# An eighth set of seven block products over x in a gated hybrid trunk: a linear-attention gate group and a merge gate are computed as a set of their own

## The chip, the cores and the metric

The kernel runs on one core of one Trainium2 chip. The metric is the device time of one execution in microseconds (us). A core has a matrix engine (TensorE, PE in the profile, with its weight loads as PEld), a vector engine (VectorE, DVE), a scalar engine (ScalarE, ACT), GpSimd (POOL) and SyncE (SP), which here only issues transfers. The engines run side by side, each works its instructions in order, and they wait for each other by semaphores. Sixteen DMA engines move data between the memory of the chip (HBM) and the on-chip memory.

## The reference, cut to what matters

One layer on x (256 tokens, 2048 channels, float32). It is a normalisation, one wide projection, two token mixers side by side, and two more projections:

```
h = rmsnorm(x, pre_norm_g)
proj = h @ w_in            # 2048 x 18448 columns
a_q, a_k, a_v, a_g, a_lr, b_q, b_k, b_v, b_g, m_a, m_b = split(proj)
gk  = log_sigmoid(a_lr @ gla_gk_w2 + gla_gk_b) / 16
o_a = rmsnorm(gla(a_q, a_k, a_v, gk)) * silu(a_g)       # linear attention, 4 heads
o_b = rmsnorm(diff_attention(b_q, b_k, b_v)) * (1 - lam_init) * silu(b_g)   # 16 heads
merged = sigmoid(m_a) * (o_a @ w_branch_a) + sigmoid(m_b) * (o_b @ w_branch_b)
out = x + rmsnorm(merged @ w_out, post_norm_g)
```

The change touches the columns a_g (the gate of linear attention, 2048 wide, four groups of 512) and m_b (the merge gate of the second branch, four groups of 512). What is computed does not change.

## The kernel before, in words

**Precision.** Every weight and every left operand is split into two float32r parts: hi, made by ScalarE, and lo, what is left over, made by VectorE. A product is the sum of three matmuls: hi with hi, lo with hi, hi with lo.

**Blocks.** `chunk_plan` lists the blocks of columns. Most are 512 columns wide: `v*` (values of linear attention), `ag0` to `ag3` (its gate), `dv*` and `bg*` (values and gate of differential attention), `m00` to `m13` (merge gates), `y*` (the two branch projections), `o*` (the output). The keys and queries (`k*`, `q*`, `dk*`, `dq*`) are 128 columns each. Weights are streamed from HBM in halves of 128 x 1024 floats (512 KB), and each half is used once.

A **plain** token-major block (`token_major`) is 8 halves; each gives 12 matmuls of 512 columns: 2 slices of the contraction, 2 halves of the tokens, 3 products. A channel-major block (`channel_major`, keys and queries) is 2 halves.

**Sets.** Two 512-column blocks can be computed together as a 2 x 2 block product with seven instead of eight block products (the scheme of Strassen and Winograd). `SETS` names the pairs, `PRODUCTS` the seven products with their operand (a quarter of x or a sum of quarters, "square"), their chain and the weight quarter that is added. A product has 4 **units**, a set 28; a unit is one half of weights and 6 matmuls (`set_product`). The sums of weight quarters are built in **chains**: buffers in the on-chip memory into which GpSimd's queue loads one quarter (L233) and then adds the next by an accumulating DMA (L232). `refill` issues each such load two units after the buffer was read. A set in `MOVED` takes the order of `ORDERS[0]`, where all chain sums are made by DMA and the quarter of p2 comes by SP; the other sets use `ORDERS[1]`, in which VectorE adds two buffers for four units after p5 (L255) and four at p2 (L260). `FULL` marks a set that loads the quarter of p2 late, by SP. Sets 0 and 1 begin with empty chains (`start_sets`); later sets are chained to the one before.

The results of a set go to `head_set` (values and gate of a group of four heads), `merge_gate` (tanh, then a store to HBM) or the output.

**Order.** `schedule` writes the order of all halves and units: `regular` puts plain blocks, `mixed(n, ...)` spreads n units evenly among the halves of the blocks named. `take` hands out the next half or unit and keeps four of them emitted ahead; hi and lo have three buffers each. Everything else is a list of **tasks** (generators: the scores and the output of linear attention, differential attention, fetches), and `pump` advances the first of them by a step after every second unit, every channel block, or every second half of a plain block (every half while `fast` is set). A planner then orders the instructions of each engine by what it expects them to cost; `keep_in_program_order` pins some. The pool `big` has 34 tiles of 4 KB a partition, shared by operands, chains, values and attention.

**Stages, by the profile's times.** v blocks, then v4 with keys and queries and set 0 (to 234 us); ag0 to ag3, with the last levels of the linear attention's scores and its output step `gla_out` (to 353); four head stages, each with 16 halves of dq and dk, units between, and differential attention (`diff_attention`) as tasks (to 669); m12 and m13; y0, the first branch (from 744); y1; o2 with the last set; o3 and the end.

`gla_out(hf)` runs once for each pair of heads of linear attention. It needs the scores, the values of its two heads (`vh`, `vl`, stored to HBM earlier and fetched by `fetch_values`) and two gate tiles (`ua`). `gates_of` and `values_of` hold the results of a head set until differential attention has used them; `weigh` waits until the set of its group is complete. After the head stages `fetch_a` brings back the operands of y0 (`oah`, `oal`).

Of the kernel before, what the change touches and what calls it, by code (L numbers as in the profile page):

```python
# [79 lines left out]
def schedule():  # L80

    kinds = {key: kind for key, kind, _, _ in chunk_plan()}
    steps = []
    blocks = [(i, n) for i in range(len(SETS)) for n in range(SLOTS * 4)]

    def regular(*keys):
        steps.extend((key, n) for key in keys for n in range(units(kinds[key])))

    def mixed(n, *keys):
        at = len(steps)  # L90
        regular(*keys)
        r = steps[at:]
        del steps[at:]
        for i, step in enumerate(r):
            steps.extend(blocks[: (i + 1) * n // len(r) - i * n // len(r)])
            del blocks[: (i + 1) * n // len(r) - i * n // len(r)]
            steps.append(step)

    def channels(g):
        return [key for key in kinds if key[:2] in ("dq", "dk") and key[2] == str(g)]  # L100

    order = [key for key, _, _, _ in chunk_plan()]
    def alone(n):
        steps.extend(blocks[:n])
        del blocks[:n]

    regular(*order[: order.index("v4")])
    mixed(SLOTS * 4, *order[order.index("v4") : order.index("ag0")])
    regular("ag0", "ag1")
    mixed(5, "ag2")  # L110
    mixed(8, "ag3")
    mixed(15, *channels(0))
    mixed(19, *channels(1))
    mixed(20, *channels(2))
    mixed(20, *channels(3))
    mixed(18, "m12", "m13")
    mixed(43, *(f"y0{g}" for g in range(4)))
    alone(4)
    mixed(16, "y10", "y11")
    regular("y12", "y13")  # L120
    mixed(SLOTS * 4, "o2")
    regular("o3")
    assert not blocks
    return steps


SLOTS = 7
SETS = (("dv0", "bg0"), ("dv1", "bg1"), ("dv2", "bg2"), ("dv3", "bg3"), ("m10", "m11"), ("m00", "m01"), ("m02", "m03"), ("o0", "o1"))
LAST = 6
OUT = 7  # L130


PRODUCTS = {
# [7 lines left out]
}  # L141


MOVED = (0, 2, 3)

FULL = (4,)
ORDERS = (("p1", "q3", "p5", "p2", "q6", "q7", "p4"), ("p1", "q3", "p5", "q6", "q7", "p2", "p4"))


# [4 lines left out]
def order_of(n):  # L154
    return OUT_ORDER if n == OUT else ORDERS[n not in MOVED]

# [9 lines left out]
def hybrid_kernel(ctx: ExitStack, tc, xt, xn, preg, postg, w, w2, gkb, glag, lamv, diffg, ident_d, causal_d, lmask_d, out):  # L166
# [107 lines left out]
    def emit_half():  # L274
        j = emitted[0]
        emitted[0] += 1
        key, unit = steps[j]
        if j in begin:
            start_sets()
        if j == begin_out:  # L280
            start_out()
        if j == begin_out + 8:
            for n in range(4):
                plain[OUT, "p2", n] = u([P, 1024], "plain")
                block(OUT, "p2", n, add=False)
        if isinstance(key, int):
            i = set_steps.index((key, unit))
            name, part = order_of(key)[unit // 4], unit % 4
            if key == 1 and part == 0 and unit < 16:
                fetch_square(PRODUCTS[order_of(key)[unit // 4 + 1]][0])  # L290
            chain, (kh, g) = chain_of(key, name), PRODUCTS[name][2]
            if (key, name, part) in plain:
                raw = plain.pop((key, name, part))
            elif chain is None:
                raw = wpool.tile([P, 1024], F32, tag="raw", name=f"raw_s{key}_{unit}", bufs=6)
                at = 1024 * (part % 2)
                sp.dma_start(raw, piece(SETS[key][g], 2 * kh + part // 2)[:, at : at + 1024])
            else:
                raw = chains[chain][part]
            hi_t = wpool.tile([P, 1024], F32R, tag="hi", name=f"hi_{j}")  # L300
            lo_t = wpool.tile([P, 1024], F32R, tag="lo", name=f"lo_{j}")
            act.activation(hi_t, raw, AF.Copy)  # L302
            dve.tensor_tensor(out=lo_t, in0=raw, in1=f32(hi_t), op=ALU.subtract)  # L303
            refill(i, key, name, part, raw)
            ready[j] = ((key, unit), hi_t, lo_t)
            return
        size = sizes[key]
        h = unit % 2
        src = piece(key, unit // 2)
        n = size // 2  # L310
        early = key == "v0"
        if j == 2:
            load_x(2, 2)
        if j == 0:
            raw = raw_0
        else:
            raw = wpool.tile([P, 1024], F32, tag="raw", name=f"raw_{key}_{unit}", bufs=6)
            i = sp.dma_start(raw[:, :n], src[:, n * h : n * h + n])
        if early:
            if j:  # L320
                tc.keep_in_program_order(i)
            if j == 0:
                load_x(1, 1)
            for kt in X_LOADS[j // 2] if h else ():
                load_x(kt, 4)
        if early:
            prep_x(j)
            if 6 <= j < 14:
                square_x(j - 6)
        if key == "o3" and j + 1 < len(steps):  # L330
            hi_t, lo_t = u([P, 1024], "keep", F32R), u([P, 1024], "keep", F32R)
        else:
            hi_t = wpool.tile([P, 1024], F32R, tag="hi", name=f"hi_{j}")
            lo_t = wpool.tile([P, 1024], F32R, tag="lo", name=f"lo_{j}")
        fine = 2 if j == 0 else 1
        for i in range(fine):
            a, b = n * i // fine, n * (i + 1) // fine
            r = raw[:, a:b]
            act.activation(hi_t[:, a:b], r, AF.Copy)  # L339
            dve.tensor_tensor(out=lo_t[:, a:b], in0=r, in1=f32(hi_t[:, a:b]), op=ALU.subtract)  # L340
        ready[j] = (key, hi_t, lo_t)
# [350 lines left out]
    def fetch_square(name):  # L692
        parts[name] = tuple(u([P, 8, P], "square", F32R) for _ in range(2))
        for t, src in zip(parts[name], parts_far[name]):
            tc.keep_in_program_order(pool.dma_start(f32(t), src))
# [76 lines left out]

    values_of, gates_of = {}, {}

    def head_set(n, src, i, b):
        g = n
        if i == 0:
            if b == 0:
                values_of[g] = u([P, 2, 512], "dv")
            act.activation(values_of[g][:, b, :], src, AF.Copy, scale=rstd[:, b : b + 1])  # L780
        else:
            if b == 0:
                gates_of[g] = u([P, 2, 512], "ub")
            gate(src, b, gates_of[g][:, b, :])

    def all_sets():
        for n in range(4):
            yield from block_set(n, lambda src, i, b: head_set(n, src, i, b))
            done.add(f"set{n}")
        yield from block_set(4, lambda src, i, b: merge_gate(1, i, b, src))  # L790
        for n in (5, 6):
            yield from block_set(n, lambda src, i, b: merge_gate(0, 2 * n - 10 + i, b, src))
        yield from out_set()

    def fetch(dst, src):
# [134 lines left out]
    def gla_out(hf, gates):  # L930
        og = []
        while f"scores{hf}" not in done:
            yield
        fetch_values(2 * hf + 1)
        for h in range(2):
            (ah, al), xh_, xl_ = att[hf], vh[2 * hf + h], vl[2 * hf + h]
            banks = [ps("bg"), ps("bg")]
# [12 lines left out]
            for b in range(2):  # L950
                dve.scalar_tensor_tensor(out=o[:, b, :], in0=banks[b], scalar=ssq[:, b : b + 1], in1=o[:, b, :], op0=ALU.mult, op1=ALU.mult)
            og.append(o)
            yield
            if h == 0 and not fast[0]:
                yield
# [18 lines left out]
    def fetch_values(h):  # L974
        vh[h], vl[h] = u([P, 2, 512], "vh", F32R), u([P, 2, 512], "vl", F32R)
        for t, far in ((vh[h], vh_far[h]), (vl[h], vl_far[h])):
            tc.keep_in_program_order((pool if h == 3 else sp).dma_start(f32(t), far))

    gates = []
    for g in range(4):  # L980
        if g % 2:
            fetch_values(g - 1)
        fast[0] = True
        banks = token_major(f"ag{g}", 512, x_ops)
        fast[0] = False
        t = u([P, 2, 512], "ua")
        for b in range(2):
            gate(banks[b], b, t[:, b, :])
        gates.append(t)
        if g % 2:  # L990
            tasks.insert(0 if f"scores{g // 2}" in done else len(tasks), gla_out(g // 2, gates[g - 1 :]))


    obh, obl = [], []
# [75 lines left out]
    def diff_attention():  # L1070

        last = pair = og = None
        n = 0
        while n < 16 or last or pair:
            new = None
            if n < 16:
# [44 lines left out]
            last = new  # L1121
            if n == 16:
                yield

    def diff_heads(g):
        obh.append(u([P, 4, S], "obh", F32R))
# [24 lines left out]

    tasks.append(diff_attention())
    diff_heads(0)
    while not {"out0", "out1"} <= done:
        pump()
    diff_heads(1)
    diff_heads(2)
    diff_heads(3)

# [14 lines left out]
            yield  # L1174

    tasks.append(fetch_a())
    for g in (2, 3):
        banks = token_major(f"m1{g}", 512, x_ops, 2)
        for b in range(2):
            merge_gate(1, g, b, banks[b])  # L1180
    while tasks:
        pump()
    for g in range(4):
# [296 lines left out]
```

## Time and profile before

| | us |
|---|---|
| median of three runs | 1098.16 |
| lowest and highest | 1097.91, 1099.25 |
| profiled execution, whole | 1099.57 |
| profiled execution, span from first to last instruction | 1097.8 |

| engine | busy us | share |
|---|---|---|
| PE | 1086.1 | 99% |
| PEld | 930.2 | 85% |
| DVE | 863.6 | 79% |
| ACT | 692.5 | 63% |
| POOL | 195.7 | 18% |

The mean granted clock of TensorE is 0.998 of full speed. The DMA queues read 266.22 MB from HBM and wrote 24.12 MB over the span.

How to read it: a row of a group names the line, the engine, the operation, output and input tiles, the shape and the count, then the busy time with the mean duration in ns, then the idle time of the engine before these instructions and what ended it. A matmul's row shows about 390 ns for 512 columns because matmuls are pipelined; the distance between their starts is what they cost when they follow each other.

### The profile page before, as it was taken

What the parts mean: (1) busy time and instruction counts of PE and PEld (TensorE: products, weight loads), DVE (VectorE), ACT (ScalarE), POOL (GpSimd) and SP (SyncE); (2) the same over time, 40 slices, a digit from 0 to 9 for tenths busy, and PEclk for the clock granted to TensorE, in tenths of its full rate; (3) what the DMA queues carried; (4) which work ended last, traced back from release to release, by engine and by line L of the source; (5) the groups of instructions that cost most, each with busy time, mean ns of one, the idle gap of its engine ahead of it and who ended that gap; (6) DMA issues with size and microseconds to landing.
All of it is one profiled execution on the core that took longest, in us unless ns stands there. A gap on an engine that the chain in (4) does not pass through costs nothing.

```text
span 1097.8 us, 15522 instructions
## 1 busy us (share of the span) xinstructions
PE 1086.1 (99%) x5504; PEld 930.2 (85%) x5504; DVE 863.6 (79%) x1193; ACT 692.5 (63%) x1009; POOL 195.7 (18%) x291
## 2 busy tenths in 40 slices
PE   9999999999999999999999999999999999999997
PEld 9999888888888888888888888788888888888886
DVE  6787668997779697877887787877778687687994
ACT  7868555655656566776766776656565666536772
POOL 0112103000211211302221211312111223201100
PEclk9999999999999999999999999999999999999999
DMA  8789989857899768989799879898787999987874
GB/s 318 257 294 332 301 278 259 314 171 269 235 359 244 268 204 233 227 234 291 220 218 307 239 219 300 224 337 305 212 236 233 328 346 349 363 307 233 209 194 149
DMA packets 83262, 291.37 MB, mean 265 GB/s; under 512 B 10032, under 2 KB 11056, under 8 KB 83184
## 3 DMA queue, kind: packets, MB, share of 16 engines
q0 software_dynamic: 34528, 124.80, 43.7%
q1 hardware_dynamic: 47792, 164.31, 42.0%
q10 hardware_dynamic: 864, 1.27, 0.3%
q8 instruction: 43, 0.70, 0.2%
q14 instruction: 35, 0.29, 0.1%
HBM read 266.22 MB, written 24.12 MB: 264 GB/s over the span
## 4 chain that ended last, share of the span: by engine, by line
PE 96%; issue 1%; DVE 1%; DMA 0%; POOL 0%; ACT 0%; DVEq 0%; POOLq 0%; SPq 0%; ACTq 0%
PE mm L510 36%; PE set L710 27%; PE mm L531 16%; PE mm L533 8%; PE bg L510 2%; PE mm L492 1%; PE bg L1012 1%; PE bg L886 1%; PE bg L492 1%; PE bg L1045 0%; PE bg L1223 0%; PE bg L1101 0%; PE bg L963 0%; DMA raw_first<-in_w_dram 0%; PE bg L1052 0%
## 5 line engine op out<-in xcount | busy, mean ns | idle before, releaser
L302 ACT ACTIVATE hi<-chain 128x1024 fp32r<-128x1024 f32 x188 | 198.9, 1059 | 158.3 <-PE mm L531 61.3
L303 DVE TENSOR_TENSOR lo<-chain,hi 128x1024 fp32r<-128x1024 f32 x188 | 229.2, 1223 | 87.3 <-ACT hi L302 85.9
L531 PE MATMUL mm<-xs,hi 128*128 128x512 f32 x768 | 198.3, 391 | 0.0
L531 PEld LDWEIGHTS mm<-xs,hi 128*128 128x128 f32 x768 | 143.4, 188 | 28.4 <-DVE oal L546 0.3
L232 POOL DMA_DIRECT2D chain<-in_w_dram x96 | 83.6, 877 | 400.9 <-DVE lo L303 257.8
L510 PE MATMUL mm<-hi,xs 128*128 128x512 f32 (+2 forms) x640 | 152.0, 377 | 0.8 <-ACT hi L339 0.8
L510 PEld LDWEIGHTS mm<-hi,xs 128*128 128x128 f32 x640 | 119.8, 190 | 16.3 <-ACT hi L339 1.1
L710 PE MATMUL set<-hi,square 128*128 128x512 f32 x448 | 122.8, 395 | 0.0
L533 PEld LDWEIGHTS mm<-xs,lo 128*128 128x128 f32 x768 | 104.7, 190 | 7.4
L533 PE MATMUL mm<-xs,lo 128*128 128x256 f32 x768 | 107.2, 282 | 0.0
L340 DVE TENSOR_TENSOR lo<-raw_y,hi 128x1024 fp32r<-128x1024 f32 x64 | 78.3, 1224 | 31.7 <-ACT hi L339 31.7
L339 ACT ACTIVATE hi<-raw_y 128x1024 fp32r<-128x1024 f32 x64 | 67.9, 1060 | 53.0 <-PE mm L510 33.9
L710 PEld LDWEIGHTS set<-hi,square 128*128 128x128 f32 x448 | 81.3, 189 | 15.9 <-ACT qk L1134 1.0
L710 PE MATMUL set<-hi,xs 128*128 128x512 f32 x336 | 92.0, 395 | 0.0
L510 PE MATMUL mm<-lo,xs 128*128 128x512 f32 (+2 forms) x320 | 82.2, 375 | 0.0
L710 PEld LDWEIGHTS set<-hi,xs 128*128 128x128 f32 x336 | 60.8, 189 | 11.7 <-ACT qk L1134 1.3
L710 PE MATMUL set<-lo,square 128*128 128x512 f32 x224 | 69.5, 391 | 0.0
L510 PEld LDWEIGHTS mm<-lo,xs 128*128 128x128 f32 x320 | 60.1, 189 | 8.1 <-DVE lo L340 0.3
L233 POOL DMA_DIRECT2D chain<-in_w_dram x64 | 35.4, 562 | 155.7 <-DVE lo L303 114.0
L339 ACT ACTIVATE hi<-raw_ag 128x1024 fp32r<-128x1024 f32 x32 | 34.0, 1061 | 33.2 <-PE mm L510 19.3
L710 PE MATMUL set<-lo,xs 128*128 128x512 f32 x168 | 51.9, 390 | 0.0
L510 PE MATMUL mm<-hi,obh 128*128 128x512 f32 x128 | 50.1, 392 | 0.0
(301 smaller groups left out, 1980.4 us busy)
## 6 DMA issues: line engine op xcount, KB each, us to landing
chain<-in_w_dram POOLq DMA_DIRECT2D x160, 512.0 KB, 8.8
raw_y<-in_w_dram SPq DMA_DIRECT2D x64, 512.0 KB, 6.7
raw_ag<-in_w_dram SPq DMA_DIRECT2D x32, 512.0 KB, 4.9
raw_dq<-in_w_dram SPq DMA_DIRECT2D x32, 512.0 KB, 6.0
raw_dk<-in_w_dram SPq DMA_DIRECT2D x32, 512.0 KB, 6.8
raw_v<-in_w_dram SPq DMA_DIRECT2D x31, 416.0 KB, 5.2
raw_k<-in_w_dram SPq DMA_DIRECT2D x16, 512.0 KB, 7.4
raw_q<-in_w_dram SPq DMA_DIRECT2D x16, 512.0 KB, 7.9
```

The lines of the kernel that those rows point to most:

```text
L232: return pool.dma_start(dst, src, accum_op=ALU.add)
L233: return queue.dma_start(dst, src)
L302: act.activation(hi_t, raw, AF.Copy)
L303: dve.tensor_tensor(out=lo_t, in0=raw, in1=f32(hi_t), op=ALU.subtract)
L339: act.activation(hi_t[:, a:b], r, AF.Copy)
L340: dve.tensor_tensor(out=lo_t[:, a:b], in0=r, in1=f32(hi_t[:, a:b]), op=ALU.subtract)
L492: i = pe.matmul(out, lhs, rhs, start=first and n == 0, stop=last and n == len(pairs) - 1)
L510: i = pe.matmul(banks[g][b][:, :n], a[part][:, P * b : P * b + P], w[:, c : c + n], start=first, stop=last)
L531: i = pe.matmul(o, hi[:, c], x_pair(kt), start=kt == 0, stop=kt == KT - 1)
L533: i = pe.matmul(o[:, :S], lo[:, c], x_ops(kt)[0], start=False, stop=False)
L710: i = pe.matmul(bank, a[part], wt[:, 512 * j : 512 * j + 512], start=go, stop=end, skip_group_check=not first)
L886: pe.matmul(o, xk[:, P * c : P * c + P], xq.rearrange("p (b c t) -> p b c t", b=2, c=4)[:, :, c, :], start=i == 0, stop=i == 1)
```

## The change

- `SETS` gets a new first pair, ("ag3", "m13"). The plain blocks ag3 and m13 disappear from the order. `first_set` takes the new set's results: the gate tile `linear_gate` for the last head of linear attention, and `merge_gate(1, 3, ...)`.
- All other sets move one place back; `LAST`, `OUT`, `MOVED` and `FULL` are renumbered with them, so that each old set keeps its order of products, and the set that is now second (dv0, bg0) begins with empty chains. The squares are fetched back for it in its own order of products.
- The order has 4 and 6 units in ag1 and ag2, 26, 28, 28, 28 in the head stages, 14 in m12 and 42 in y0, instead of 5 and 8 in ag2 and ag3, 15, 19, 20, 20, then 18 in m12 and m13, and 43.
- `gla_out(1)` is queued after ag2. It fetches the values of head 2 itself, takes two more steps before it uses them, and fetches those of head 3 (on GpSimd's queue) only after head 2 is done.
- `diff_attention` does not start before both halves of linear attention have their output; the loop that forced this after the first head stage is gone. After the last scores it takes one more step.

```diff
@@ schedule
-    regular("ag0", "ag1")
-    mixed(5, "ag2")
-    mixed(8, "ag3")
-    mixed(15, *channels(0))
-    mixed(19, *channels(1))
-    mixed(20, *channels(2))
-    mixed(20, *channels(3))
-    mixed(18, "m12", "m13")
-    mixed(43, *(f"y0{g}" for g in range(4)))
+    regular("ag0")
+    mixed(4, "ag1")
+    mixed(6, "ag2")
+    mixed(26, *channels(0))
+    mixed(28, *channels(1))
+    mixed(28, *channels(2))
+    mixed(28, *channels(3))
+    mixed(14, "m12")
+    mixed(42, *(f"y0{g}" for g in range(4)))
@@
-SETS = (("dv0", "bg0"), ("dv1", "bg1"), ("dv2", "bg2"), ("dv3", "bg3"), ("m10", "m11"), ("m00", "m01"), ("m02", "m03"), ("o0", "o1"))
-LAST = 6
-OUT = 7
+SETS = (("ag3", "m13"), ("dv0", "bg0"), ("dv1", "bg1"), ("dv2", "bg2"), ("dv3", "bg3"), ("m10", "m11"), ("m00", "m01"), ("m02", "m03"), ("o0", "o1"))
+LAST = 7
+OUT = 8
-MOVED = (0, 2, 3)
-FULL = (4,)
+MOVED = (0, 1, 3, 4)
+FULL = (5,)
@@ emit_half
-            if key == 1 and part == 0 and unit < 16:
-                fetch_square(PRODUCTS[order_of(key)[unit // 4 + 1]][0])
+            if key == 1 and part == 0 and unit < 24:
+                ahead = PRODUCTS[order_of(key)[unit // 4 + 1]][0]
+                if ahead in parts_far:
+                    fetch_square(ahead)
@@
+    linear_gate = []
+
+    def first_set(src, i, b):
+        if i:
+            merge_gate(1, 3, b, src)
+            return
+        if b == 0:
+            linear_gate.append(u([P, 2, 512], "ua"))
+        gate(src, b, linear_gate[0][:, b, :])
@@ all_sets
-        for n in range(4):
-            yield from block_set(n, lambda src, i, b: head_set(n, src, i, b))
-            done.add(f"set{n}")
-        yield from block_set(4, lambda src, i, b: merge_gate(1, i, b, src))
-        for n in (5, 6):
-            yield from block_set(n, lambda src, i, b: merge_gate(0, 2 * n - 10 + i, b, src))
+        yield from block_set(0, first_set)
+        for g in range(4):
+            yield from block_set(g + 1, lambda src, i, b: head_set(g, src, i, b))
+            done.add(f"set{g}")
+        yield from block_set(5, lambda src, i, b: merge_gate(1, i, b, src))
+        for n in (6, 7):
+            yield from block_set(n, lambda src, i, b: merge_gate(0, 2 * n - 12 + i, b, src))
@@ gla_out
-        fetch_values(2 * hf + 1)
+        fetch_values(hf + 1)
+        if hf:
+            yield
+            yield
...
             og.append(o)
+            if h == 0 and hf:
+                fetch_values(3)
             yield
@@
-    for g in range(4):
-        if g % 2:
-            fetch_values(g - 1)
+    for g in range(3):
+        if g == 1:
+            fetch_values(0)
...
-        if g % 2:
-            tasks.insert(0 if f"scores{g // 2}" in done else len(tasks), gla_out(g // 2, gates[g - 1 :]))
+        if g:
+            tasks.insert(0 if f"scores{g - 1}" in done else len(tasks), gla_out(g - 1, gates[:2] if g == 1 else (gates[2], linear_gate[0])))
@@ diff_attention
+        while "out1" not in done:
+            yield
         while n < 16 or last or pair:
...
             if n == 16:
                 yield
+                yield
@@
     diff_heads(0)
-    while not {"out0", "out1"} <= done:
-        pump()
     diff_heads(1)
+    assert {"out0", "out1"} <= done
...
-    for g in (2, 3):
-        banks = token_major(f"m1{g}", 512, x_ops, 2)
-        for b in range(2):
-            merge_gate(1, g, b, banks[b])
+    banks = token_major("m12", 512, x_ops, 2)
+    for b in range(2):
+        merge_gate(1, 2, b, banks[b])
```

More of the change, by code (lines that the diff above doesn't have):

```diff
@@ L773, in hybrid_kernel, with head_set @@
     values_of, gates_of = {}, {}
-    def head_set(n, src, i, b):
-        g = n
+    linear_gate = []
[6 more added lines that the diff above has]
+        gate(src, b, linear_gate[0][:, b, :])
+    def head_set(g, src, i, b):
         if i == 0:
```

## The prediction

> **What bounds the kernel now.** I read the page first: busy shares and the chain that ended last.
>
> ```profile
> span 1097.8 us, 15522 instructions
> ...
> PE 1086.1 (99%) x5504; PEld 930.2 (85%) x5504; DVE 863.6 (79%) x1193; ACT 692.5 (63%) x1009; POOL 195.7 (18%) x291
> ...
> PE 96%; issue 1%; DVE 1%; DMA 0%; POOL 0%; ACT 0%; DVEq 0%; POOLq 0%; SPq 0%; ACTq 0%
> ```
>
> TensorE is busy for 99% of the span and is 96% of the chain. Its waits on other engines, with their total, number and longest, are few:
>
> ```profile
> PE bg L1101 <- DVE ogb L1068: 1.4, 1, 1.4
> PE bg L425 <- DVE ones L422: 1.1, 1, 1.1
> PE mm L510 <- ACT hi L339: 0.8, 1, 0.8
> ```
>
> So what counts is how many matmuls are issued and how far apart. The chain in order of time gives the distance:
>
> ```profile
> 710.40 2.72 PE mm L510 x12
> ...
> 737.60 2.72 PE set L710 x12
> ...
> 1083.34 7.33 issue
> ```
>
> Twelve 512-column matmuls take 2.72 us in a plain block and in a set alike: 0.2267 us each. The 7.33 us at the end follow the last product and are not touched.
>
> The third view is the time by stretch: four head stages, then the block m12, then the branch stage y0, y1, and the stage of the last set (busy time of each engine, granted clock, share of the 16 DMA engines, GB/s).
>
> ```profile
> core 0: us, PE busy (x) PEld busy (x) DVE busy (x) ACT busy (x) POOL busy (x), PEclk, DMA share, GB/s
> 353.50:427.90 74.40, 74.40 (x410) 63.58 (x409) 61.39 (x97) 47.34 (x78) 12.54 (x21) 1.00 0.75 248
> 427.90:503.00 75.10, 75.10 (x426) 64.30 (x425) 58.05 (x122) 51.38 (x99) 16.90 (x20) 1.00 0.91 234
> 503.00:583.00 80.00, 80.00 (x452) 68.58 (x451) 64.64 (x131) 54.25 (x103) 19.07 (x27) 1.00 0.89 240
> 583.00:669.00 86.00, 86.00 (x483) 73.64 (x482) 67.36 (x130) 58.61 (x107) 17.17 (x24) 1.00 0.88 252
> 669.00:706.00 37.00, 37.00 (x187) 30.58 (x186) 32.17 (x64) 25.23 (x51) 5.69 (x6) 1.00 0.83 255
> 744.00:886.00 142.00, 142.00 (x627) 117.40 (x626) 104.99 (x92) 86.18 (x92) 28.36 (x45) 1.00 0.87 268
> 896.00:957.00 61.00, 61.00 (x270) 50.48 (x269) 45.44 (x42) 34.98 (x36) 17.16 (x29) 1.00 1.03 345
> 1015.00:1067.00 52.00, 52.00 (x231) 42.79 (x230) 51.74 (x55) 40.57 (x49) 6.79 (x8) 1.00 0.83 203
> ```
>
> TensorE is full in every row. The last row matters most: VectorE is at 51.74 of 52.00 us and TensorE still loses nothing, so a VectorE share in the nineties is no loss in itself.
>
> **The main term.** A plain 512-column block is 8 halves of 12 matmuls, so ag3 and m13 are 2 x 96 = 192. A set is 28 units of 6, or 168. The change removes 24: 24 x 0.2267 = **5.44 us**, all on the path. Every other matmul stays and only changes place.
>
> The Trainium skill, page "TensorE: Matmul & The Clock Gate", section "Back-to-back issue gap", states a sustained spacing of about 131 ns at 512 columns; by it the term would be an estimated 3.1 us. The trace disagrees with its 0.2267 us.
>
> **What the set adds beside TensorE.** 28 halves are split into hi and lo instead of 16, so 12 more of each of these:
>
> ```profile
> L302 ACT ACTIVATE hi<-chain 128x1024 fp32r<-128x1024 f32 x188 | 198.9, 1059 | 158.3 <-PE mm L531 61.3
> L303 DVE TENSOR_TENSOR lo<-chain,hi 128x1024 fp32r<-128x1024 f32 x188 | 229.2, 1223 | 87.3 <-ACT hi L302 85.9
> ...
> L232 POOL DMA_DIRECT2D chain<-in_w_dram x96 | 83.6, 877 | 400.9 <-DVE lo L303 257.8
> ```
>
> ACT gets 12 x 1.06 = 13 us, VectorE 12 x 1.22 = 15 us and six sums of a bank, about 4 us; GpSimd 24 more issues of at most 0.88 us, 21 us. Shares become 65%, 81% and 20%. SP loses 16 loads and gains four. All of this is hidden on average; the question is where it bunches. The new set itself runs where the first set runs now, with the same 28 units among the same blocks. Each later set starts one place later, and the plain blocks that are gone leave more units for the head stages: 26, 28, 28, 28 instead of 15, 19, 20, 20, and 14 beside the one block m12 instead of 9.
>
> The split's share of VectorE in two of the stretches:
>
> ```profile
> 503.00:583.00 80.00, 43.14 (x37) 1.00 0.89 240
> ...
> 669.00:706.00 37.00, 19.41 (x17) 1.00 0.83 255
> ```
>
> 37 splits take 43.14 us, 1.17 each; the rest of VectorE there is 64.64 - 43.14 = 21.5 us. With 44 halves (16 + 28) the stage has 80 + 7 x 1.36 = 89.5 us of TensorE and 64.64 + 7 x 1.17 = 72.8 us of VectorE, 81%. The stage of heads 1 also gets the eight chain sums of the unmoved set dv1, which now falls there:
>
> ```profile
> L255 DVE TENSOR_TENSOR chain<-chain,chain 128x1024 f32<-128x1024 f32 x4 | 4.9, 1218 | 0.0
> ```
>
> 8 x 1.22 = 9.8, with 1.5 us for the larger part of a set's own sums: 84.1 of 89.5 us, 94%. In m12 (17 halves become 22): TensorE 37 + 5 x 1.36 + about 1 us of attention's end = 44.8; VectorE 32.17 + 5 x 1.14 + two more chain sums 2.4 + the set's sums and attention's end, some 3.6 = 43.9, 98%. Both lie below the 99.5% that costs nothing between 1015 and 1067 us. Attention works beside them, though, in bursts. Bounds: 0, and 7.2 us (the first rival). I take 0.5, nearer to the rows in which TensorE is full.
>
> **The linear attention's end.** It comes into the first head stage, without ag3 to cover it. The values of head 2 are now fetched when the output step begins, two task steps ahead of their product. Those steps are worth about 6.8 us there (three units of 1.36 and a half of 2.72), and such loads land after:
>
> ```profile
> DMA to landing us min/median/max: 5.0/7.4/9.7
> ```
>
> TensorE works in order, so it would wait between 0 and 9.7 - 6.8 = 2.9 us, once; the matmul may also have been placed later by the planner. I take 0.5. Attention now waits for this output. Counted task step by task step with 2.72 us a half and 1.36 us a unit, the output is complete some 11 us later than now, and the first scores only 3 us later, since more units mean more steps. From then on each head's set ends ahead of the first product that needs it, so that wait stays empty.
>
> **m12 and the start of y0.** In the trace m12 starts at 668.97 and the plain m13 gives room behind it:
>
> ```profile
> 668.97 1.98 PE L510 MATMUL mm<-hi,xs 128*128 128x512 f32 x8
> ...
> 708.42 0.59 PE L1101 MATMUL bg<-ident,ogb 128*128 128x128 f32 x2 [1.43 <-DVE ogb L1068]
> ...
> 744.24 0.39 PE L510 MATMUL mm<-hi,oah 128*128 128x512 f32 x1
> ```
>
> Attention ends 39.5 us after m12's start, y0 begins after 75. Now m12 alone lasts 8 x 2.72 + 14 x 1.36 = 40.8 and some 4 us of attention, so y0 begins at about 45, and its fifth load, which first needs the third and fourth fetched operand, at 45 + 4 x (2.72 + 1.31 x 1.36) = 63. These are SP's fetches (start and length of each, then landing):
>
> ```profile
> 696.74 0.37 SPq L796 DMA_DIRECT2D oah<-oah_far  x1
> ...
> 708.65 0.32 SPq L796 DMA_DIRECT2D oal<-oal_far  x1
> ...
> DMA to landing us min/median/max: 9.9/12.3/22.3
> ```
>
> 28 to 40 us after m12's start, landed by 52 at the median and 62 at worst: just in time. Behind a late fetch on SP stand the weight halves of y0. Bounds: -1.4 (the wait at 708 goes) and +5; I take 0.2.
>
> **Transfers.** The bytes moved now:
>
> ```profile
> DMA packets 83262, 291.37 MB, mean 265 GB/s; under 512 B 10032, under 2 KB 11056, under 8 KB 83184
> ```
>
> Twelve more halves of 512 KB are 6.3 MB, 2%. A chain's buffer is refilled eight units later: 8/28 x 89.5 = 25.6 us in the head stages, against 8/43 x 142 = 26.4 in y0, whose row shows TensorE full. Landing of chain loads:
>
> ```profile
> DMA to landing us min/median/max: 3.8/8.8/21.0
> ```
>
> I take 0 here.
>
> **Sum.** -5.44 + 0.5 + 0.5 + 0.2 = -4.2 us on the profiled execution: its span 1097.8 becomes 1093.6. It took 1099.57 us as a whole, 1.4 above the median of the three runs; I put the difference on the median: 1098.16 - 4.2 = **1093.9**.
>
> **Rivals.** *VectorE bunches at the chain sums.* While four units carry a sum each, the head stage has 4 x 1.36 + 2.29 x 2.72 = 11.7 us of TensorE and (8 + 2.29) x 1.22 + 0.27 x 11.7 = 15.7 us of VectorE: 4.0 too much. Now, in m12 (3.56 halves to four units), it is (8 + 3.56) x 1.22 + 0.21 x 15.1 = 17.3 against 4 x 1.36 + 3.56 x 2.72 = 15.1: 2.2 too much, and no wait shows there until 708. Beyond 2.2 it could cost 1.8, at four places (twice in heads 1, twice at m12): 7.2 us, **1099.9**; with nothing absorbed 16, 1108.7. Against it: the hi and lo buffers run two units ahead, and not every sum is urgent.
>
> *A late fetch* of values or operands at both of the places above: 2.9 + 5 - 0.7 on the forecast, **1101** at worst, 1097 at half.
>
> *Transfers become the bound of the head stages*, the case on the other side. Each of heads 1 to 3 must move 44 halves and two stores of 0.52 MB, 24.1 MB in 89.5 us: 270 GB/s. Heads 0 moves 42 and some 12 other such tiles (values in, operands in and out), 28.3 MB in 74.4 + 11 x 1.36 + about 5 us of linear attention = 94 us: 301 GB/s. If 234 / 0.91 = 257 GB/s were the ceiling, these stages would take 93.8 and 110 us: 3 x 4.3 + 16 = 29 us, **1122**. It decides from the point where the rate stays below 270. Against it: 345 GB/s between 896 and 957 us with TensorE full. The Trainium skill, page "Perfetto Trace Analysis", section "Identifying the Most-Contended Engine", says that occupancy misleads for the DMA engines and bytes should be judged; by this the share of 0.91 is no ceiling. The trace agrees with its 1.03 at 345 GB/s.
>
> *More is won*: the wait of 1.4 us goes and nothing comes, 1098.16 - 5.44 - 1.4 = 1091.3.
>
> **How the numbers follow.** Forecast 0.62 (1092 to 1095.9); bunching 0.17, of it 0.05 beyond 1100.4; late fetch 0.07; transfers 0.09; more won 0.05. A measurement of this kernel tells about 0.2%, 2.2 us, from no change. Faster: 0.62 + 0.05 = 0.67. Same: 0.12 + 0.07 = 0.19. Slower: 0.05 + 0.09 = 0.14. The range runs from 1091.3 to 1100.0, which leaves out transfers and the worst bunching.
>
> **What would show it.** Matmuls 5480 instead of 5504; TensorE's busy time down by 5.4 us; 12 matmuls at 2.72 us as now; TensorE full in heads 1 and m12 with VectorE above 90%; no wait of TensorE on vh or oah. I am wrong if TensorE's waits in the head stages or around y0's start sum to over 3 us, or if the chain leaves TensorE for DMA or VectorE there.

## The result and the profile after

The changed kernel takes 1109.52 us (median of 4 runs, 1106.76 to 1111.48) against 1098.70 us for the kernel before on the same chip: a ratio of 1.0093, interval 1.0079 to 1.0107. It is slower by 10.8 us. The forecast was 1093.9, faster by 4.2, with a range that ended at 1100.0.

The page of the changed kernel, its span, busy shares and the chain that ended last:

```profile
span 1108.2 us, 15525 instructions
...
PE 1085.6 (98%) x5480; PEld 925.9 (84%) x5480; DVE 879.0 (79%) x1211; ACT 708.6 (64%) x1023; POOL 217.9 (20%) x315
...
PE 38%; DVE 2%; issue 1%; ACT 1%; DMA 0%; DVEq 0%; POOLq 0%; POOL 0%; ACTq 0%
```

The 24 matmuls are gone (5480 instead of 5504), and the shares of the other engines lie within two points of the ones worked out beforehand (79%, 64% and 20% against 81%, 65% and 20%). Yet the busy time of TensorE fell by 0.5 us only, not by 5.4. So two things happened: TensorE waited more, and while it was busy, it was slower somewhere. The named engines of the chain now sum to 42% of the span, so the time is read from the waits and the stretches instead.

The waits of TensorE in the changed kernel (total, number, longest):

```profile
PE set L712 <- ACT p L729: 4.0, 1, 4.0
PE mm L533 <- ACT hi L341: 3.5, 5, 0.9
PE bg L494 <- DMA vl<-vl_far: 3.0, 1, 3.0
PE bg L427 <- DVE ones L424: 1.1, 1, 1.1
PE mm L512 <- ACT hi L341: 1.0, 2, 0.7
PE set L712 <- ACT hi L304: 0.6, 1, 0.6
PE mm L535 <- DVE lo L342: 0.6, 2, 0.4
```

Three rows are new and large. None of the three names VectorE.

**First, the fetch of values.** TensorE in the output step `gla_out(0)`, then the queue of SP at the same place, both from the timeline (start, length):

```profile
294.50 0.61 PE L712 MATMUL set<-hi,square 128*128 128x512 f32 x2
298.14 0.50 PE L494 MATMUL bg<-vl,ath 128*128 128x512 f32 x1 [3.03 <-DMA vl<-vl_far]
...
299.25 0.63 PE L494 MATMUL bg<-vh,atl 128*128 128x512 f32 x1
299.68 0.63 PE L494 MATMUL bg<-vh,ath 128*128 128x512 f32 x1
```

```profile
289.93 0.33 SPq L994 DMA_DIRECT2D vh<-vh_far  x1
290.35 0.38 SPq L994 DMA_DIRECT2D vl<-vl_far  x1
```

The values of head 1 are fetched at 290, and the second of the two transfers lands 7.7 us after its issue, at 298. SP's own waits say why it was not issued earlier:

```profile
SPq L994 <- PE bg L494: 2.9, 1, 2.9
```

SP waited until TensorE had read head 0's values: there was no free tile in the pool. In the kernel before these two loads went out at 276.6 and 277.1, ahead of the matmuls of head 0, which began at 283.6.

**Second, the copy of a set's product.** ScalarE and TensorE in m12, from the timeline:

```profile
713.72 0.50 ACT L1047 ACTIVATE prob<-prob,mx,score_scale 128x128 f32<-128x128 f32 x1 [0.27 <-DVE mx L1042]
...
714.47 1.07 PE L512 MATMUL mm<-lo,xs 128*128 128x512 f32 x4
...
718.84 0.18 ACT L1047 ACTIVATION_READ_ACCUMULATOR prob<-prob,mx,score_scale 128x1 f32 x1
718.93 0.57 ACT L729 ACTIVATE p<-set 128x512 f32<-128x512 f32 x1
719.55 2.08 PE L712 MATMUL set<-hi,square 128*128 128x512 f32 x4 [4.02 <-ACT p L729]
721.43 1.05 PE L712 MATMUL set<-lo,square 128*128 128x512 f32 x2
```

In the order of a set that is not moved, q6 follows p5 directly and accumulates on p5's bank, after ScalarE has copied that bank out (L729). ScalarE has the exponentials of two heads ahead of this copy, from 713.72 to 718.93, with one split among them. TensorE stands still for 4.0 us.

**Third, the first operand of a half in the head stages**, at one of five places:

```profile
481.21 0.49 ACT L1047 ACTIVATE prob<-prob,mx,score_scale 128x128 f32<-128x128 f32 x1 [0.61 <-DVE mx L1042]
...
486.34 0.19 ACT L1047 ACTIVATION_READ_ACCUMULATOR prob<-prob,mx,score_scale 128x1 f32 x1
486.43 1.04 ACT L341 ACTIVATE hi<-raw_dq 128x1024 fp32r<-128x1024 f32 x1
487.53 1.66 PE L533 MATMUL mm<-xs,hi 128*128 128x512 f32 x6 [0.67 <-ACT hi L341]
```

Again the exponentials of two heads, 5.2 us with one split between, stand ahead of what TensorE needs next.

The waits alone do not make up the loss. The stretches around the first two show the rest (busy time of each engine, granted clock of TensorE, share of the DMA engines, GB/s):

```profile
core 0: us, PE busy (x) PEld busy (x) DVE busy (x) ACT busy (x) POOL busy (x), PEclk, DMA share, GB/s
298.00:302.00 4.00, 3.86 (x10) 3.04 (x11) 0.03 (x1) 1.38 (x4) 0.00 (x0) 0.57 0.91 205
714.00:719.50 5.50, 1.54 (x7) 0.94 (x5) 4.58 (x16) 5.50 (x18) 0.00 (x0) 0.90 0.81 207
719.50:727.00 7.50, 7.45 (x21) 5.93 (x22) 3.20 (x4) 2.98 (x4) 0.00 (x0) 0.62 0.19 69
```

After each long wait the clock is down: 0.57 over 4.0 us, 0.62 over 7.5 us. Matmuls that were 0.2267 us apart are now 0.43 apart (299.25 to 299.68). That loses 4.0 x 0.43 = 1.7 us and 7.5 x 0.38 = 2.9 us on top of the waits. With them the fetch costs 3.0 + 1.7 = 4.7 us and the copy 4.0 + 2.9 = 6.9 us. What is to be explained is 10.8 + 5.4 = 16.2 us.

One difference between the two profiled executions has nothing to do with the change. The first 356 matmuls are the same, in the same order, in both kernels. The matmul that comes next (L577, now L579) starts at 71.82 us in the kernel before and at 69.91 in the changed one. In the profiled executions of the experiments below the same matmul starts between 69.64 and 71.82 us. So two single executions can differ by 2.2 us before the change has had any effect, and spans of single executions are compared with that in mind.

### The profile page after: what moved, and what is told of

The parts are those of the page before. It is cut to its first block, busy times and chain, and to the rows that moved or that the text cites. A ratio compares the mean times of both kernels' runs of the same rounds, so it can differ in the third digit from the quotient of the medians.

```text
span 1108.2 us, 15525 instructions
## 1 busy us (share of the span) xinstructions
PE 1085.6 (98%) x5480; PEld 925.9 (84%) x5480; DVE 879.0 (79%) x1211; ACT 708.6 (64%) x1023; POOL 217.9 (20%) x315
## 5 line engine op out<-in xcount | busy, mean ns | idle before, releaser
L305 DVE TENSOR_TENSOR lo<-chain,hi 128x1024 fp32r<-128x1024 f32 x212 | 257.4, 1223 | 72.6 <-ACT hi L304 72.1
L304 ACT ACTIVATE hi<-chain 128x1024 fp32r<-128x1024 f32 x212 | 223.5, 1058 | 130.6 <-PE set L712 48.7
L533 PE MATMUL mm<-xs,hi 128*128 128x512 f32 x768 | 199.3, 392 | 3.5 <-ACT hi L341 3.5
L232 POOL DMA_DIRECT2D chain<-in_w_dram x112 | 97.4, 870 | 435.4 <-DVE lo L305 292.3
L533 PEld LDWEIGHTS mm<-xs,hi 128*128 128x128 f32 x768 | 142.6, 188 | 32.8 <-ACT hi L341 5.6
L712 PE MATMUL set<-hi,square 128*128 128x512 f32 x512 | 142.3, 399 | 4.0 <-ACT p L729 4.0
L512 PE MATMUL mm<-hi,xs 128*128 128x512 f32 (+2 forms) x512 | 119.3, 372 | 1.0 <-ACT hi L341 1.0
L512 PEld LDWEIGHTS mm<-hi,xs 128*128 128x128 f32 x512 | 94.8, 188 | 12.1 <-ACT hi L341 1.6
L342 DVE TENSOR_TENSOR lo<-raw_y,hi 128x1024 fp32r<-128x1024 f32 x64 | 78.3, 1224 | 28.6 <-ACT hi L341 27.7
L233 POOL DMA_DIRECT2D chain<-in_w_dram x72 | 39.5, 563 | 151.3 <-DVE lo L305 134.4
L512 PE MATMUL mm<-lo,xs 128*128 128x512 f32 (+2 forms) x256 | 64.7, 369 | 0.0
L712 PEld LDWEIGHTS set<-lo,square 128*128 128x128 f32 x256 | 48.8, 191 | 11.1 <-DVE lo L305 0.2
L342 DVE TENSOR_TENSOR lo<-raw_dk,hi 128x1024 fp32r<-128x1024 f32 x32 | 39.1, 1222 | 22.7 <-ACT hi L341 22.7
L341 ACT ACTIVATE hi<-raw_dk 128x1024 fp32r<-128x1024 f32 x32 | 33.9, 1058 | 30.9 <-PE mm L533 29.3
```

The source lines that it names most:

```text
L232: return pool.dma_start(dst, src, accum_op=ALU.add)
L233: return queue.dma_start(dst, src)
L512: i = pe.matmul(banks[g][b][:, :n], a[part][:, P * b : P * b + P], w[:, c : c + n], start=first, stop=last)
L533: i = pe.matmul(o, hi[:, c], x_pair(kt), start=kt == 0, stop=kt == KT - 1)
L712: i = pe.matmul(bank, a[part], wt[:, 512 * j : 512 * j + 512], start=go, stop=end, skip_group_check=not first)
```

## The experiments

Theory: the saving of 5.4 us is there, and three waits (fetch, copy, first operand) eat it, the two long ones doubled by the clock. The rivals: the transfers of the head stages, or VectorE, bind; or the fuller stages lose in many small places that no single edit gives back. All edits are to the changed kernel unless said. Ratios are to the kernel before.

**The values are used two task steps later.**

```diff
@@ gla_out, after the step of a head
+            if h == 0 and not hf:
+                yield
+                yield
```

> The changed kernel with two more task steps in the first output of linear attention between its first and its second head, so that the values of head 1 are used about 5 us later; the fetch stays where it is. Theory (TensorE waits 3.0 us for this fetch and then runs at about half its clock for some 4 us): both go, 4.9 us less than the changed kernel, 1104.6, with granted clock 1.00 around that product. Rival (the wait only hides another one, of VectorE or of the tiles): within 1 us of 1109.5.

1104.16 us, ratio 1.0048 (1.0033 to 1.0063). The wait on vl is gone and that on the copy stays at 4.0. The median falls by 5.4 us, for a wait of 3.0: the rest fits the 1.7 us of slow clock, within the scatter of the runs. In the profiled execution the load was issued at 290.9 and landed 5.2 us later, and the product began at 298.7; a landing of 7.7 us would just have been in time as well.

**The task step after the last unit of p1 and p5 comes behind the copy**, so that the exponentials queue up behind it.

```diff
-            if unit % 2:
+            if unit % 2 and not (late and unit == 3):
                 pump()
@@ block_set, p1 and p5
                 act.activation(kept, bank, AF.Copy)
+                pump()
```

> The changed kernel, but after the last unit of p1 and p5 the copy of the bank stands ahead of the next task step instead of behind it. Theory (at m12 the product q6 waits 4.0 us for ScalarE's copy of p5, which stands behind the exponentials of two heads, and then runs at half the clock): the copy stands ahead of the second head's four exponentials (2.1 us), the wait falls to about 2, the slow stretch gets shorter or goes: 2 to 6 us less, 1103.5 to 1107.5. Rival (ScalarE is too full at m12 whatever the order): the wait moves to the next split, 1109.5.

1103.00 us, ratio 1.0043 (1.0028 to 1.0057). The wait is halved, not gone, since the four exponentials of the first head and a split still lie ahead of the copy. The waits and the stretch behind:

```profile
PE set L712 <- ACT p L729: 1.9, 1, 1.9
...
PE bg L494 <- DMA vl<-vl_far: 0.6, 1, 0.6
```

```profile
716.60:721.00 4.40, 4.31 (x12) 3.40 (x13) 3.12 (x6) 3.18 (x11) 0.00 (x0) 0.61 0.25 74
```

A wait of 1.9 us still brings the clock to 0.61 for 4.4 us, that is 1.7 us more. The fetch was late by 0.6 us only in this execution: its transfer landed 5.7 us after issue, not 7.7. So this run mixes two gains and its 6.5 us cannot all be put down to the copy.

**Set 5 takes the order of the moved sets**, in which p2 stands between p5 and q6, and all its chain sums are made by DMA.

```diff
-MOVED = (0, 1, 3, 4)
+MOVED = (0, 1, 3, 4, 5)
```

> The changed kernel with set 5 (m10, m11) among the moved sets: p2 stands between p5 and q6, so q6 does not need the copy at once; eight sums of VectorE go, eight accumulating loads come. Theory: wait and slow stretch at m12 go, 7 us less, 1102.5. Rival (transfers bind at m12): 4.2 MB more there, at 270 GB/s up to 15 us more, 1110 to 1125.

1100.87 us (10 runs), ratio 1.0018 (1.0008 to 1.0027). The wait on the copy is gone. The fetch was late by 1.8 us here, and the clock did not fall behind it:

```profile
298.70 0.50 PE L494 MATMUL bg<-vl,ath 128*128 128x512 f32 x1 [1.76 <-DMA vl<-vl_far]
```

```profile
298.70:301.00 2.30, 2.30 (x10) 1.91 (x11) 0.00 (x0) 1.00 (x3) 0.36 (x1) 1.00 0.99 301
```

Set 5 gives more transfers and less VectorE work in this form. That it is faster speaks against the transfers as the bound, and leaves VectorE open as a second reason at this place.

**Sixteen matmuls whose result nobody uses, put ahead of q6 of set 5.** They keep TensorE at work while it would wait, and add 16 x 0.2267 = 3.6 us of work. Nothing else is changed.

```diff
+                if n == 5:
+                    spare = ps("bg")
+                    for _ in range(16):
+                        pe.matmul(spare, x_ops(0)[0][:, :P], x_pair(0), start=True, stop=True)
                 yield from product_of(name, b5, False)
```

> The changed kernel with 16 matmuls more, whose result nobody uses, put ahead of q6 of set 5: 3.6 us of work on TensorE where it waits 4.0 us. Theory (the idle time itself lowers the clock): the copy ends as before, but the 18 matmuls behind it run at full clock, so about 3 us less than the changed kernel in spite of more work, 1106.5, granted clock 1.00 there. Rival (the slow matmuls have another cause, such as their operands): no gain, 1109.5 or some 3 us more.

1104.29 us, ratio 1.0054 (1.0035 to 1.0072): with more work the kernel is 5.2 us faster. The stretches of this run:

```profile
712.00:716.00 4.00, 4.00 (x19) 3.28 (x18) 3.36 (x13) 3.98 (x15) 0.00 (x0) 1.00 1.06 282
716.00:722.00 6.00, 6.00 (x28) 4.80 (x27) 4.04 (x7) 4.50 (x7) 0.00 (x0) 1.00 0.22 64
```

TensorE is full and its clock stays at 1.00. Work in place of the wait should leave 6.9 - 3.6 = 3.3 us. The other 1.9 us are within what the fetch does from one execution to the next: it was late by 0.6 us in this profiled execution instead of 3.0, and no slow clock followed. This run shows the slow clock as a consequence of the wait, not of the place.

**The later use and the moved set 5 together.**

```diff
-MOVED = (0, 1, 3, 4)
+MOVED = (0, 1, 3, 4, 5)
@@ gla_out
+            if h == 0 and not hf:
+                yield
+                yield
```

> Both repairs at once: the later use of the values of head 1 and set 5 among the moved sets. Theory (the two long waits with their slow stretches are separate, and add up): 1100.9 less the 2 us and slow matmuls that were left at the fetch, 1097 to 1098.5; what is left above 1093.7 are the five waits on ScalarE in the head stages. Rival (more transfers now bind): as with set 5 alone, 1101.

1099.07 us (10 runs), ratio 0.9997 (0.9988 to 1.0007): both long waits are gone and the kernel stands where it stood before the change. It gains 1.8 us on the moved set alone, as much as that one's wait on the fetch in its profiled execution. The largest row left among the waits is the third one:

```profile
PE mm L533 <- ACT hi L341: 3.4, 5, 0.9
```

**A step between two heads' exponentials**, on top of that.

```diff
                     exponents(new)
                     yield
                     diff_weights(new)
+                    if n < 14:
+                        yield
                     exponents(second)
```

> The kernel with both repairs and one task step more between the exponentials of the two heads of a pair (not for the last pair). Theory (the five waits of 0.5 to 0.9 us for a split on ScalarE come from eight exponentials close together, 5.8 us, while units stand two for one): they go, 4 us less than with both repairs, 1093 to 1095. Rival (ScalarE and VectorE are too full on average in the head stages): the waits move, no change.

1093.67 us, ratio 0.9949 (0.9934 to 0.9964). The waits of L533 are gone. ScalarE at the place shown above, now with the split in front of the second head's exponentials:

```profile
478.54 1.04 ACT L304 ACTIVATE hi<-chain 128x1024 fp32r<-128x1024 f32 x1
479.48 1.04 ACT L341 ACTIVATE hi<-raw_dq 128x1024 fp32r<-128x1024 f32 x1
480.43 0.48 ACT L1050 ACTIVATE prob<-prob,mx,score_scale 128x128 f32<-128x128 f32 x1
```

The step is worth 5.4 us by the medians, 2 us more than the five waits sum to. The traces place part of these 2 us. A wait is counted from the modelled end of the matmul before it, and the distance of the starts shows more: at the place shown above the last two matmuls of the unit start from 486.25 on, so the next could start at 486.25 + 2 x 0.2267 = 486.70, and it starts at 487.53, 0.83 us late where the wait says 0.67. By distances the five places cost 4.3 us in the run before this one and nothing here. The other 1.1 us are not placed, but they are less than what the start of an execution can make: the matmul of L579 starts at 71.39 us in the profiled execution of the run before and at 70.12 in this one.

**The same step in the kernel before the change.** The edit is the one above, made to the kernel before.

> The kernel before with the step between the two heads' exponentials alone. Theory (with 15 to 20 units a stage the splits never came late, so there is nothing to win): within 0.2% of before, 1097 to 1101. Rival (the step helps by itself): 1094.

1098.92 us (10 runs), ratio 0.9996 (0.9987 to 1.0005): nothing. So the step is no gain of its own; it takes away something that the change had brought.

**Four units moved from the last head stage to m12**, with the later use and set 5 in its old order.

```diff
-    mixed(28, *channels(3))
-    mixed(14, "m12")
+    mixed(24, *channels(3))
+    mixed(18, "m12")
```

> The changed kernel with the later use of the values, set 5 unmoved again, and four units moved from the last head stage to m12 (24 and 18 instead of 28 and 14). Theory (the wait at m12 is a coincidence of place: p5 of set 5 ends as the exponentials of the last pair stand on ScalarE): p5 then ends two weight halves later, behind them, and the 4.0 us and the slow stretch go without any change of work: 7 us less than with the later use alone, 1097 to 1098. Rival (VectorE at 98% is the cause at m12): 18 units with their sums are worse there, over 1104.

1096.39 us (10 runs), ratio 0.9975 (0.9965 to 0.9985). The wait on the copy is gone without a new order of products. In the trace the copy (709.97) now stands between the exponentials of the two heads (703.92 and 710.88), and TensorE works on a half of m12 (from 709.26) until it is done. Two of the five waits of L533 are gone as well (2.1 us in three places). The set still uses VectorE for its sums, and this stretch of m12 tests VectorE as a bound:

```profile
700.00:712.00 12.00, 12.00 (x60) 9.58 (x57) 11.97 (x30) 8.81 (x19) 2.99 (x4) 1.00 0.89 173
```

VectorE is busy for 11.97 of 12.00 us and TensorE for all of them.

**With the step between the heads added to that**, nothing else:

> The changed kernel with the later use of the values, four units moved from the last head stage to m12, and the step between the two heads' exponentials; set 5 unmoved. Theory (all three causes are gone, and no transfer is added): 1096.4 less the 2 to 3 us of the three waits on ScalarE that are left, 1093 to 1094; TensorE's waits in the head stages under 1 us in all. Rival (something else is left): 1096.

1093.43 us, ratio 0.9950 (0.9937 to 0.9962), the same as with the moved set. Two ways of removing the copy's wait end at one time.

**Fewer units in a head stage**: 22 in each, with 8 and 16 in ag1 and ag2 and 50 in y0, the later use and the moved set 5, without the step between the heads.

```diff
-    mixed(4, "ag1")
-    mixed(6, "ag2")
-    mixed(26, *channels(0))
+    mixed(8, "ag1")
+    mixed(16, "ag2")
+    mixed(22, *channels(0))
@@ heads 1 to 3: 22 instead of 28 each
-    mixed(42, *(f"y0{g}" for g in range(4)))
+    mixed(50, *(f"y0{g}" for g in range(4)))
```

> Both repairs, and the units spread otherwise: 8 and 16 in ag1 and ag2, 22 in each head stage instead of 26 to 28, 50 in y0 instead of 42. Theory (two units for each half make the head stages sensitive to ScalarE's bursts): the five waits go, 4 us less than with both repairs, 1093 to 1095. Rival (the linear attention's tasks in ag1 and ag2 suffer in their place, or y0 does): no gain or a loss, 1097 to 1102.

1112.52 us, ratio 1.0116 (1.0098 to 1.0134): the slowest of all. The waits of L533 are gone, and others have come:

```profile
PE bg L494 <- DMA vl<-vl_far: 3.3, 2, 3.1
PE set L712 <- ACT hi L304: 2.8, 2, 1.6
PE bg L1065 <- DVE prob L1060: 2.1, 1, 2.1
PE set L712 <- DVE lo L305: 1.5, 1, 1.5
PE bg L1032 <- DVE obl L548: 1.2, 1, 1.2
```

The order of the units also sets when every task gets its step, so this edit moved the fetch, the attention and the splits together. It fits the theory in that the waits of L533 go with fewer units in a stage, but what the density of units costs by itself cannot be read from it. It also shows that here VectorE can make TensorE wait, in three of the rows.

**One more tile in the pool** `big` (35), one fewer for incoming weights (5), nothing else changed.

```diff
-    big = ctx.enter_context(tc.tile_pool(name="big", bufs=34))
+    big = ctx.enter_context(tc.tile_pool(name="big", bufs=35))
@@ three places
-                 ... bufs=6)
+                 ... bufs=5)
```

> The changed kernel with 35 instead of 34 tiles in the large pool, paid for by five instead of six buffers for the raw weight halves. Theory (the fetch of the values of head 1 starts only when TensorE has read head 0's, because no tile is free): it starts some 5 us earlier, the wait of 3.0 us and its slow stretch go, 1104 to 1106. Rival (the landing itself is slow): the fetch starts as late as now, 1109, and more if five buffers are too few.

1108.39 us, ratio 1.0096 (1.0079 to 1.0112), runs from 1103.16 to 1111.77. SP's queue in the profiled execution, the one of 1103.16 us:

```profile
281.98 0.42 SPq L994 DMA_DIRECT2D vh<-vh_far  x1
...
289.67 0.33 SPq L994 DMA_DIRECT2D vl<-vl_far  x1
```

The first transfer goes out 8 us earlier, so a free tile is what it had waited for. There are two tiles to fetch, though, and the second waits as before. It landed 4.6 us after issue here; a weight load of TensorE waited 0.6 us for it, and its matmuls lost 0.3 us. The wait on the copy is 4.0 us as before, but less slow clock follows it than the 2.9 us lost in the changed kernel:

```profile
714.80:722.30 7.50, 7.49 (x26) 6.09 (x27) 4.01 (x5) 3.18 (x3) 0.00 (x0) 0.77 0.23 70
```

That is 7.5 x 0.23 = 1.7 us. In the three other executions (1108 to 1112 us) the load may have landed later; they have no trace. Their mean granted clock is 0.994, against 0.997 here, so TensorE had more time at half clock in them. As a remedy the tile fails; as a test of the reason it answers for one transfer of the two.

**All sets up to 5 in the moved order**, with the later use and the step between the heads. No chain sum falls to VectorE in these sets, and the transfers are the heaviest of all runs.

```diff
-MOVED = (0, 1, 3, 4)
+MOVED = (0, 1, 2, 3, 4, 5)
```

> The later use of the values, the step between the exponentials, and sets 2 and 5 both among the moved sets: no chain sum of VectorE is left before y0 but eight more accumulating loads of 512 KB stand in head stage 1. Theory of bunched chain sums (they cost TensorE something in head stage 1, where two waits of 0.2 and 0.4 us for VectorE remain): 0.5 us less than with set 5 moved alone, 1093.2. Rival (transfers bind): 4.2 MB more in head stage 1, up to 10 us more.

1092.84 us, ratio 0.9943 (0.9930 to 0.9955), the fastest of all, although its difference to the two other good ones (0.6 and 0.8 us) is within their scatter. Its head stages 0 and 1:

```profile
353.00:430.00 77.00, 77.00 (x412) 65.71 (x411) 62.49 (x96) 51.99 (x80) 20.42 (x29) 1.00 1.00 287
430.00:505.00 75.00, 75.00 (x423) 64.06 (x422) 63.11 (x130) 55.27 (x106) 21.25 (x27) 1.00 0.91 255
```

TensorE is full at a DMA share of 1.00 and 287 GB/s.

## Why the prediction was wrong, point by point

**The main term held.** 24 matmuls less, 0.2267 us each. With the three kinds of wait taken away the kernel lands at 1093.67, 1093.43 and 1092.84 us, where the sum had put it (1093.9). These versions are 5.4 to 6.2 us below the kernel before, whose own wait of 1.4 us at 708 is gone in them too. That they end within 1.1 us of the forecast is partly chance, since the forecast did not count on that wait to go and added 1.2 us for losses.

**The step that failed is "All of this is hidden on average; the question is where it bunches".** The question was right, and it was then asked of VectorE alone. VectorE's bursts cost next to nothing in the changed kernel: 0.6 us of waits for L342; and there are none in m12 with four units more (f3), at 11.97 of 12.00 us. ScalarE, at 65%, was counted once and let go. It works in order, and a task step hands it the exponentials of two heads at once, 5.2 us with a split among them. What counts is not its share but what stands behind that burst in its queue: a copy that the next product needs (4.0 us), and a split that the next half needs (3.5 us as waits, 4.3 by distances, 5.4 by the run that removes it). With more units between the halves, these instructions came to lie behind the bursts. In m12 the prediction worked out VectorE's share to 98% and did not ask what q6 waits for.

**The fetch of values was put at the wrong place, and its size came out by coincidence.** Its bound was "between 0 and 9.7 - 6.8 = 2.9 us, once"; the wait is 3.0, once. But it is head 1 in the first output step, not head 2 in the second, because the free tile, not the two steps, set the time of issue; head 2 made TensorE wait nowhere. The 0.5 taken for it counted on the planner to place the product later, and no row supported that.

**Every wait was priced at its own length.** In the profiled execution the two long ones cost 4.7 and 6.9 us instead of 3.0 and 4.0. The range had no room for that: 2.9 us at worst for the fetch, 7.2 for bunching at four places.

**The start of y0** gave no wait on the fetched operands; 0.2 us was enough. **Transfers** were rightly taken at 0: the rival put the ceiling at 257 GB/s, and the run with all sets moved has 287 with TensorE full. **The rival of bunching at the chain sums** comes near the result in number (1108.7 with nothing absorbed) and is wrong in kind: moving set 5's sums to DMA and leaving them on VectorE, with four units moved, end at the same time (1093.67 and 1093.43).

**The sum as it turned out**, in us: -5.4 for the matmuls, +4.7 fetch, +6.9 copy, +5.4 bursts in the head stages, -1.4 for the wait that went: +10.2, against 10.8 measured. It mixes waits of one execution with a difference of medians. By the traces alone the bursts are 4.3, and two small new rows (L304 and L342) come to 1.2: +10.3. The profiled execution of the changed kernel is 10.4 us longer than that of the kernel before although its start was 1.9 us shorter, so some 2 us of its loss are not placed. The prediction's own condition, over 3 us of waits in the head stages or around y0's start, came true.

## What to carry to other kernels

An engine that is busy for two thirds of the time can still set the pace if its work comes in bursts: for each instruction that the bounding engine will wait for, ask what stands ahead of it in its own engine's queue at the moment it is needed. A wait of a few microseconds on a matrix engine that is otherwise full should be priced at more than its length: here waits of 1.9, 3.0 and 4.0 us cost 3.6, 4.7 and 6.9. Where a change moves work between stages, the interleaving changes for everything that is driven by it; here an order of units that was fuller by design became 5 to 6 us faster than before only after edits of a few lines had given the fetch more time and taken the dependent instructions out from behind the bursts.

## What was not expected of the hardware

The clock reacts to short waits. Waits of 1.9, 3.0 and 4.0 us were followed by half speed: 4.4 us at 0.61, 4.0 us at 0.57 and 7.5 us at 0.62 lose 1.7, 1.7 and 2.9 us, which is about 3.4, 3.4 and 5.7 us at half speed. Behind the 4.0 us another 1.1 us at half speed (5.50 us at 0.90) lie ahead of the first matmul, 6.8 us in all; behind the same wait in the run with one tile more it is 3.4. The length of a wait alone does not decide. A wait of 1.8 us (e3) left the clock at 1.00. In the run with fewer units a wait of 1.2 us at 701.6 was followed by half speed, and one of 2.1 us at 460.2 was not:

```profile
704.40:707.80 3.40, 3.40 (x9) 2.63 (x8) 2.24 (x9) 2.68 (x8) 0.00 (x0) 0.50 1.04 276
458.00:466.00 8.00, 5.94 (x37) 4.96 (x37) 7.96 (x24) 7.51 (x22) 1.11 (x2) 1.00 0.48 144
```

The Trainium skill, page "TensorE: Matmul & The Clock Gate", section "What's actually happening", says that activity is judged in free-running windows of about 3.4 us and that the clock after an idle one is half. The traces agree with the half, and with 3.4 us, once or twice, as the length of a slow stretch. They do not agree that a whole window must be idle: 1.9 us without matmuls were enough, and 1.2 us in one place.

The landing time of one and the same load near 290 us was 7.7, 6.5, 5.7, 5.4, 5.2 and 4.6 us in six profiled executions of neighbouring kernels. Where the product followed at once (the first four), TensorE's wait was 3.0, 1.8, 0.6 and 0.6 us. Why it differs was not settled. The four runs of the version with one tile more, which needs this load at once, lie 8.6 us apart, the five of the fastest version, which uses it later, 2.1 us. That the late load makes all of this scatter is not shown; the start (2.2 us) and the length of the slow stretch behind the copy's wait differ between executions as well.
